# A row softmax bound by DMA: narrow loads of the first tile against a split load of the third

## The chip, the core and the metric

The kernel runs on one core of a Trainium2 chip. The metric is device time in microseconds of one execution. The core has a vector engine (DVE), a scalar engine (ACT), a sync engine (SP) that here issues every transfer, and sixteen DMA engines that all of SP's transfers share.

## The reference

A softmax with temperature over the last axis of a 16 x 256 x 32768 float32 array:

```python
def setup_inputs():
    batch, seq, vocab = 16, 256, 32768
    return {
        "logits": np.random.randn(batch, seq, vocab).astype(np.float32),
        "temperature": 1.0,
    }

def reference(logits: np.ndarray, temperature: float) -> np.ndarray:
    scaled = logits / temperature
    scaled = scaled - scaled.max(axis=-1, keepdims=True)
    exp_scaled = np.exp(scaled)
    return (exp_scaled / exp_scaled.sum(axis=-1, keepdims=True)).astype(np.float32)
```

512 MB are read and 512 MB are written.

## The kernel before

The 4096 rows of 32768 values are seen as 8192 half rows of 16384, so that a tile is 128 half rows, one to a partition, 64 KB each (8 MB in all), and two neighbouring partitions hold one row. There are 64 tiles and three buffers (`_BUFS`) for them in the on-chip memory `xs`; tile g uses buffer g mod 3, and it is loaded, worked on in place and stored from there.

**Work on a tile.** A tile is cut along its columns into three pieces of 6304, 5376 and 4704 columns (`_PLAIN`), the last two tiles into six (`_LATE`). `Work.vector` takes the negated maximum of each piece on DVE (L207). `Work.scalar` then does the exponential of each piece with that maximum as bias, and sums it (L267). A few small operations on DVE and ACT exchange maxima and sums between the two partitions of a row and make one factor per piece. The pieces are scaled with it, the first one on ACT (L286), the other two on DVE (L258).

**Order.** The program orders everything by hand with semaphores; no scheduler is involved. SP runs one list of loads and stores, written by `order`: load 0, 1, 2, store 0, load 3, store 1, store 2, then load i and store i-1 in turn, and at the end load 62, load 63, store 61, 62, 63. In front of a load into a buffer in use, SP waits until the store from that buffer has landed; in front of a store it waits for the scaling. SP issues in order, and what it issues goes through one queue to the sixteen DMA engines. Tiles 4 to 60 run on DVE and ACT in a loop over three buffers; the first four and the last three tiles are written out.

**Parts of transfers.** `load_parts` cuts the load of a tile by columns. Tile 0 is loaded in two parts: 15360 columns for all 128 partitions in one transfer (rows of 60 KB), and the last 1024 columns (`_NARROW`, 4 KB a row) in nineteen narrow transfers, given by `narrow_rows`: 18 transfers of seven partitions each (every 18th row) and one of the two rows left over. Tile 3 is loaded in two halves, since tile 0 is stored in two halves (`store_parts`); the last tile is stored in three parts. All other loads and stores are one transfer of 128 rows of 64 KB.

**Waits on loads.** Each transfer adds 16 to a semaphore of its part and buffer. `landed` waits on it before the first piece that touches a part: for part 1 of tile 0 the count of all nineteen narrow transfers. As the first and the fourth tile share the semaphore of part 1, the wait for tile 3 counts past those nineteen.

Of the kernel before, what the change touches and what calls it, by code (L numbers as in the profile page):

```python
# [8 lines left out]
_W = 16384  # L9
# [1 line left out]
_PLAIN = ((6304, 5376, 4704), (0,))  # L11
_LATE = ((4096, 3072, 3072, 2048, 2048, 2048), (3, 4, 5))
_LAST_STORES = ((0, 4096), (4096, 6144), (10240, 6144))
_NARROW = 1024
_FEW = 7
_HEAD = 4
_TAIL = 3

# [45 lines left out]


def load_parts(g):
    if g == 0:
        return [(0, _W - _NARROW), (_W - _NARROW, _NARROW)]
    if g == 3:
        return [(0, _W // 2), (_W // 2, _W // 2)]  # L70
    return [(0, _W)]


def store_parts(g, n):
    if g == 0:
        return [(0, _W // 2), (_W // 2, _W // 2)]
    return list(_LAST_STORES) if g == n - 1 else [(0, _W)]


def narrow_rows(p):  # L80
    step = p // _FEW
    return [slice(q, step * _FEW, step) for q in range(step)] + [slice(step * _FEW, p)]


def order(n):
# [7 lines left out]
def kernel(  # L93
# [6 lines left out]
    nc = tc.nc  # L100
    inv_t = 1.0 / float(temperature)
    P = nc.NUM_PARTITIONS
# [8 lines left out]
    x = xf.rearrange("n (h v) -> (n h) v", h=2)  # L111
# [8 lines left out]
    X = nc.alloc_sbuf_tensor("xs", [P, _BUFS * _W], fp32)  # L120
# [4 lines left out]
    sig = Signals(nc)  # L125
    stored = {}

    def load(g):
        p = Place(g, G)
        rows = slice(g * P, (g + 1) * P)  # L130
        for j, (s, n) in enumerate(load_parts(g)):
            if g >= _BUFS:
                parts = store_parts(g - _BUFS, G)
                for i, (a, m) in enumerate(parts):
                    if a < s + n and s < a + m:
                        nc.sync.wait_ge(*stored[g - _BUFS][i])
            where = slice(p.slot * _W + s, p.slot * _W + s + n)
            key = ("ld", j, *p.key)
            if g == 0 and j == 1:
                for some in narrow_rows(P):  # L140
                    sig.dma(key, nc.sync.dma_start(out=X[some, where], in_=x[some, s : s + n]))
            else:
                sig.dma(key, nc.sync.dma_start(out=X[:, where], in_=x[rows, s : s + n]))

# [19 lines left out]
    class Work:  # L164
# [25 lines left out]
        def landed(self, engine, k, seen):  # L190
            s, n = self.p.pieces[k]
            for j, (a, m) in enumerate(load_parts(self.p.g)):
                if a < s + n and s < a + m and j not in seen:
                    seen.add(j)
                    times = len(narrow_rows(P)) if self.p.g == 0 and j == 1 else 1
                    value = self.p.n16
                    if self.p.g == 3 and j == 1:
                        value, times = 16 * len(narrow_rows(P)) + 16, 1
                    engine.wait_ge(sig[("ld", j, *self.p.key)], value * times)

        def vector(self):
            t, e, r, tv, f, K = self.t, self.e, self.r, self.tv, self.j, self.K
# [85 lines left out]
    for what, g in order(G):  # L288
        if what == "L":
            load(g)  # L290
        else:
            store(g)
# [47 lines left out]
```

## Time and profile before

| | before |
|---|---|
| median of 3 runs | 2486.93 us (2486.84 to 2486.94) |
| profiled execution | 2486.8 us, its span 2485.0 us |
| DVE busy | 1526.2 us (61%) |
| ACT busy | 1325.7 us (53%) |
| DMA queue | 19264 packets, 1073.75 MB, 99.8% of sixteen engines |
| mean rate over the span | 432 GB/s |

The span is the time from the first to the last instruction that the profile shows; the execution's own time is some 2 us longer. The DMA share is the time that packets took, as a share of sixteen engines' time. In the rows of windows the columns are: the stretch and its length in us, the busy time of DVE, ACT and POOL with numbers of instructions, the TensorE clock (not used here), the DMA share and GB/s. A packet is one row's contiguous piece, carried by one DMA engine, and is counted in a window by its start, so that short windows scatter. In the rows of the timeline the columns are the start, the length, the engine, the line, the operation, and in brackets the idle time before it with what ended it.

### The profile page before, as it was taken

How to read it: one execution, taken by the hardware profiler on the slowest of the kernel's cores; microseconds unless marked ns; L12 is line 12 of the kernel's file. 1: busy time of each engine (PE TensorE's matmuls, PEld its weight loads, DVE VectorE, ACT ScalarE, POOL GpSimd, SP SyncE). 2: the span in 40 equal slices, each digit the busy share in tenths (PEclk: the TensorE clock that was granted, in tenths of full speed). 3: DMA queues.
4: the chain of work that ended last, by engine and by line, in shares of the span. 5: the costliest groups of instructions: out<-in, count | busy, mean ns of one | idle time of the engine just before them, and what ended most of it. 6: DMA issues, size and time to landing. Idle time of an engine off the chain costs nothing.

```text
span 2485.0 us, 1689 instructions
## 1 busy us (share of the span) xinstructions
DVE 1526.2 (61%) x776; ACT 1325.7 (53%) x529; POOL 0.2 (0%) x4
## 2 busy tenths in 40 slices
DVE  5845665666656656566565665656656566566665
ACT  4744645546546455464554645546455464554654
POOL 0000000000000000000000000000000000000000
DMA  9999999999999999999999999999999999999998
GB/s 399 438 439 432 429 438 437 430 434 437 437 427 437 437 434 429 438 438 429 434 437 436 428 437 438 433 430 438 437 428 436 437 435 428 438 437 434 430 438 381
DMA packets 19267, 1073.78 MB, mean 432 GB/s; under 512 B 2240, under 2 KB 2240, under 8 KB 2368
## 3 DMA queue, kind: packets, MB, share of 16 engines
q1 hardware_dynamic: 19264, 1073.75, 99.8%
q14 instruction: 3, 0.02, 0.0%
HBM read 536.87 MB, written 536.87 MB: 432 GB/s over the span
## 4 chain that ended last, share of the span: by engine, by line
DMA 61%; DVE 28%; ACT 7%; issue 2%; SPq 0%; DVEq 0%
DMA xs<-in_logits_dram 59%; DVE t L207 21%; ACT xs L267 6%; DVE xs L258 6%; DMA out_dram<-xs 3%; SPq L160 0%; ACT ee L278 0%; DVE junk L252 0%; DVE t L225 0%; DVE row L249 0%; ACT xs L286 0%; DVE row L229 0%; DVE junk L236 0%; DVEq L299 0%; DVEq L223 0%
## 5 line engine op out<-in xcount | busy, mean ns | idle before, releaser
L267 ACT ACTIVATE xs<-xs,t 128x6304 f32<-128x6304 f32 (+5 forms) x198 | 932.1, 4707 | 1053.6 <-DVE t L207 1046.8
L207 DVE TENSOR_REDUCE t<-xs 128x1 f32<-128x6304 f32 (+5 forms) x198 | 1110.0, 5663 | 618.5 <-DMA xs<-in_logits_dram 618.5
L286 ACT ACTIVATE xs<-xs,junk 128x6304 f32<-128x6304 f32 (+1 forms) x68 | 355.6, 5236 | 45.0 <-DVE junk L252 45.0
L258 DVE TENSOR_SCALAR xs<-xs,junk 128x5376 f32<-128x5376 f32 (+2 forms) x130 | 358.8, 2803 | 2.3
L225 DVE LOAD_MASK_SELECT t<-t x64 | 0.9, 14 | 282.9 <-ACT xs L267 282.9
L278 ACT ACTIVATE ee<-t,row 128x6 f32<-128x6 f32 (+1 forms) x64 | 19.2, 300 | 35.3 <-DVE row L229 35.3
L267 ACT ACTIVATION_READ_ACCUMULATOR xs<-xs,t 128x1 f32 x198 | 37.0, 187 | 0.0
L236 DVE CUSTOM_DVE_ANT_1 junk<-ee,t 128x6 f32<-128x6 f32 (+1 forms) x64 | 10.7, 167 | 23.5 <-ACT ee L278 23.5
L252 DVE TENSOR_SCALAR junk<-ee,row 128x3 f32<-128x3 f32 (+1 forms) x64 | 14.6, 229 | 2.2
L249 DVE RECIPROCAL row<-row 128x1 f32<-128x1 f32 x64 | 10.5, 164 | 2.2
L229 DVE TENSOR_REDUCE row<-t 128x1 f32<-128x6 f32 (+1 forms) x64 | 10.2, 159 | 2.2
L225 DVE STREAM_SHUFFLE t<-t 128x6 f32<-128x6 f32 (+1 forms) x64 | 10.4, 163 | 0.5
L236 DVE DVE_READ_ACCUMULATOR2_ANT row<- 128x1 f32 x64 | 5.3, 83 | 0.0
L267 ACT ACT_TABLE_LOAD x1 | 1.3, 1283 | 0.9 <-SPq L119 0.9
L321 POOL MEMSET const-bfloat16-1.0<- 128x1 bf16 x1 | 0.1, 102 | 0.0
L321 POOL MEMSET const-uint8-127<- 128x1 uint8 x1 | 0.1, 102 | 0.0
L321 POOL MEMSET const-float32-0.0<- 128x1 f32 x1 | 0.1, 99 | 0.2 <-issue 0.2
L321 POOL MEMSET const-float32-1.0<- 128x1 f32 x1 | 0.1, 99 | 0.0
## 6 DMA issues: line engine op xcount, KB each, us to landing
out_dram<-xs SPq DMA_DIRECT2D x2, 4096.0 KB, 29.2
xs<-in_logits_dram SPq DMA_DIRECT2D x2, 4096.0 KB, 19.3
xs<-in_logits_dram SPq DMA_DIRECT2D x1, 7680.0 KB, 21.1
out_dram<-xs SPq DMA_DIRECT2D x2, 3072.0 KB, 19.5
out_dram<-xs SPq DMA_DIRECT2D x1, 2048.0 KB, 12.2
xs<-in_logits_dram SPq DMA_DIRECT2D x62, 48.1
out_dram<-xs SPq DMA_DIRECT2D x62, 29.1
xs<-in_logits_dram SPq DMA_DIRECT2D x18, 28.0 KB
```

The source lines that it names most:

```text
L207: m = v.tensor_reduce(out=t[:, k : k + 1], in_=self.piece(k), axis=mybir.AxisListType.X, op=A.max, negate=True,)
L225: v.stream_shuffle(out=t[:, 2 * K : 4 * K], in_=t[:, 0 : 2 * K], mask=swap), "sh"
L229: v.tensor_reduce(out=r[:, 0:1], in_=tv[:, :, 0, :], axis=mybir.AxisListType.XY, op=A.min),
L236: v.tensor_tensor_reduce(out=f[:, 0 : 2 * K].rearrange("p (a k) -> p a k", a=2), in0=self.ev, in1=tv[:, :, 1, :], scale=1.0, scalar=0.0, o ...
L249: self.done(v.reciprocal(out=r[:, 2:3], in_=r[:, 1:2]), "rc")
L252: v.tensor_scalar_mul(out=f[:, 0:K], in0=e[:, 0:K], scalar1=r[:, 2:3]), "f"
L258: v.tensor_scalar_mul(out=xs, in0=xs, scalar1=f[:, k : k + 1]), k, self.p.own
L267: s = a.activation(out=xs, in_=xs, func=Exp, bias=t[:, k : k + 1], scale=inv_t, accum_out=t[:, K + k : K + k + 1],)
L278: a.activation(out=self.ev, in_=self.tv[:, :, 0, :], func=Exp, bias=r[:, 0:1], scale=-1.0),
L286: self.scaled(a.mul(out=xs, in_=xs, mul=f[:, k : k + 1]), k, self.p.on_act)
L321: nc = _bacc.Bacc("TRN2", target_bir_lowering=False, num_devices=1)
```

## The change

The whole of tile 0 is loaded in one transfer of 128 rows of 64 KB. Tile 2 is loaded in ten transfers in place of one: the left half of its columns for all 128 partitions in one transfer (rows of 32 KB); the right half in seven transfers of 16 partitions each (partitions r, r+8, r+16, ... for r from 0 to 6) and two of 8 partitions each (7, 15, ..., 63 and 71, 79, ..., 127). The first eight of them count as part 0, the last two as part 1, and each part has its semaphore. The maximum of tile 0 waits for the one transfer; the first piece of tile 2 waits for all ten. With the nineteen narrow transfers gone, the wait for part 1 of tile 3 is a plain 16.

```diff
-_NARROW = 1024
-_FEW = 7
+_SPLIT = 2
...
 def load_parts(g):
-    if g == 0:
-        return [(0, _W - _NARROW), (_W - _NARROW, _NARROW)]
+    if g == _SPLIT:
+        return [(0, _W), (0, _W)]
     if g == 3:
         return [(0, _W // 2), (_W // 2, _W // 2)]
     return [(0, _W)]
...
-def narrow_rows(p):
-    step = p // _FEW
-    return [slice(q, step * _FEW, step) for q in range(step)] + [slice(step * _FEW, p)]
...
             key = ("ld", j, *p.key)
-            if g == 0 and j == 1:
-                for some in narrow_rows(P):
-                    sig.dma(key, nc.sync.dma_start(out=X[some, where], in_=x[some, s : s + n]))
+            if g == _SPLIT:
+                half = _W // 2
+                b = p.slot * _W
+                parts = [(slice(0, P), 0)] + [(slice(r, P, 8), half) for r in range(7)]
+                if j == 1:
+                    parts = [(slice(7, P // 2, 8), half), (slice(P // 2 + 7, P, 8), half)]
+                for some, c in parts:
+                    sig.dma(
+                        key,
+                        nc.sync.dma_start(
+                            out=X[some, b + c : b + c + half], in_=x[rows, c : c + half][some]
+                        ),
+                    )
             else:
                 sig.dma(key, nc.sync.dma_start(out=X[:, where], in_=x[rows, s : s + n]))
...
                     seen.add(j)
-                    times = len(narrow_rows(P)) if self.p.g == 0 and j == 1 else 1
-                    value = self.p.n16
-                    if self.p.g == 3 and j == 1:
-                        value, times = 16 * len(narrow_rows(P)) + 16, 1
-                    engine.wait_ge(sig[("ld", j, *self.p.key)], value * times)
+                    value = 16 if j == 1 else self.p.n16
+                    value = [128, 32][j] if self.p.g == _SPLIT else value
+                    engine.wait_ge(sig[("ld", j, *self.p.key)], value)
```

## The prediction

> **What bounds the kernel now.** I read the page first: engine shares, DMA line, queue line.
>
> ```profile
> span 2485.0 us, 1689 instructions
> DVE 1526.2 (61%) x776; ACT 1325.7 (53%) x529; POOL 0.2 (0%) x4
> ...
> q1 hardware_dynamic: 19264, 1073.75, 99.8%
> ```
>
> No compute engine is near full; the one DMA queue fills 99.8% of sixteen engines' time. So the time is bytes through the DMA engines, plus what slows a packet, plus how unevenly the sixteen finish. The windows show where the first loss lies.
>
> ```profile
> 2.00:62.00 60.00, 35.02 (x14) 25.39 (x10) 0.00 (x0) 1.00 1.00 409
> 62.00:139.00 77.00, 59.99 (x35) 57.46 (x24) 0.00 (x0) 1.00 1.01 435
> ```
>
> The last column is GB/s. The first three loads run at 409, everything later at 435: 60 us x 26/435 = 3.6 us is lost before 62 us, and hardly anything after it. The windows of the end show the second loss.
>
> ```profile
> 2470.00:2477.00 7.00, 0.00 (x0) 0.00 (x0) 0.00 (x0) 1.00 1.04 446
> 2477.00:2478.00 1.00, 0.00 (x0) 0.00 (x0) 0.00 (x0) 1.00 0.40 172
> 2478.00:2480.00 2.00, 0.00 (x0) 0.00 (x0) 0.00 (x0) 1.00 0.40 172
> 2480.00:2482.00 2.00, 0.00 (x0) 0.00 (x0) 0.00 (x0) 1.00 0.12 49
> ```
>
> The column before GB/s is the DMA share. It falls to 0.40 and then 0.12 while the last bytes go out: nine engines are done near 2477.5, six between 2479.9 and 2481.3, one at 2483.3.
>
> For more I went to the trace's packet records (start, duration, size). They carry no engine number, but each packet starts 3 to 4 ns before another one ends, so they string into sixteen chains:
> - A 65536-byte packet takes 2418 ns, in nearly every case exactly; a 32768-byte one 1213 (512 of them, 1227 at most); a lone 4096-byte one 159; the 4-byte semaphore write behind each transfer 9. That fits 8 ns plus 36.8 ns per KB, and leaves 3.6 us per engine above the fit in all: 0.65 in the first packet of each engine, 2.45 between 21 and 34 us, 0.5 elsewhere.
> - The 2.45 us are the narrow stretch. The 128 packets of 4096 bytes lie on just seven chains, 18 or 19 on each. The first take 159 ns, then 250 to 340, and the nine other chains, which are already reading tile 1, need 3882 to 4279 ns for a 64 KB packet in that time. All returns to 2418 soon after the narrow ones end at 26 us.
> - The seven chains leave it some 2.9 us behind the nine, and this lag stays to the end, unchanged to some ns from tile to tile. One of the seven loses another 20 ns or so per transfer, 3.2 us up to the last ones, in steps of 3 to 11 ns a packet. This late engine is the one that ends at 2483.3 us, and 1.7 us later the span ends.
>
> So the kernel ends when the late engine has done its own packets; it is never idle between. The profiled execution took 2486.8 us for its span of 2485.0 (1.8 around it); the median of the runs is 2486.93, 0.1 more.
>
> **The change, part by part**, on the late engine's chain.
>
> *Bytes moved between engines.* Before, it carries 18 narrow packets and their semaphore writes, 18 x (159 + 5) = 2.95 us, less 8 x (2418 - 2267) = 1.21 us for tile 0's shorter main packets (61440 bytes): 1.74 us above a plain load. After, tile 2 gives every engine eight packets of 32 KB for the first half and one from each of the seven 16-row transfers; the two 8-row transfers have eight packets each. Few-row transfers of the trace all went to the same chains (the 18 of seven rows to the same seven, the one of two rows to two of them), so I put both on one group of eight that contains the seven. An engine of this group has 17 pieces: 9681 ns for the first eight with their semaphore write (the spacing of tile 3's halves) and 9 x 1214 = 10926, in all 20607 against 19317 for a plain load: 1.29 above. Difference: **-0.45 us**.
>
> [...]
>
> *The slow stretch.* On the seven chains it costs 18 x (265 - 159) = 1.9 us in the narrow packets and about 0.4 in the first packets of tile 1 behind them, 2.3 us. No 4096-byte piece is left. The new pieces are 32 KB; the nearest row is tile 3's half loads and tile 0's half stores at 1213 to 1227 ns, so I price their slowdown at nothing. The far bound is the worst factor of the stretch, 4200/2418 = 1.7 on all nine added pieces: 9 x 1213 x 0.7 = +7.6 us. Below nothing is excluded, 1213 being the lowest of 512. Tile 1 behind tile 0 may keep the 20 ns a packet that tile 0's later packets show above the fit: 0.15 us. So **-2.15 us**.
>
> *Issue on SP.* It goes from one DMA, nineteen narrow ones and two to two and ten.
>
> ```profile
> 0.96 0.38 SPq L143 DMA_DIRECT2D xs<-in_logits_dram  x1
> 1.41 13.83 SPq L141 DMA_DIRECT2D xs<-in_logits_dram  x19
> 15.28 0.82 SPq L143 DMA_DIRECT2D xs<-in_logits_dram  x2
> 50.84 0.82 SPq L160 DMA_DIRECT2D out_dram<-xs  x2
> ```
>
> Nineteen at 0.73 us become ten at no more than that: all is issued by 9 us, while tile 0's packets run to 22 us and tile 2's start near 41. Nothing waits for it, before or after: 0.
>
> *Tile 0 is waited for whole.* The first maximum on DVE now needs 64 KB a row in place of 60.
>
> ```profile
> 22.09 17.34 DVE L207 TENSOR_REDUCE t<-xs 128x1 f32<-128x6304 f32 x3 [22.09 <-DMA xs<-in_logits_dram]
> ```
>
> Eight packets of 2418 in place of 2267, less a little: DVE starts 0.9 us later, and as tiles 0 to 3 follow each other on DVE without a gap, the first stores come 0.9 us later: the pair at 50.84 becomes 51.8. The cover is the queue: the leading engines are busy with tile 2 until 62.0 us now and 59.8 then. That leaves 8 us; tile 2's store at 108 keeps 8 of about 11. With the cover gone the 0.9 us would be paid in full. Tile 2's own pieces are all waited for together, but DVE reaches that tile long after it has landed: 0.
>
> *The end.* The final stores are issued at 2457.04, a fixed chain of work after tile 62 has landed on the late engine. The leading nine stood idle for up to 0.39 us there; the late one had over 5 us of its own packets in hand. The chain moves with the late engine: 0.
>
> Sum: -0.45 - 2.15 = -2.6 us. Made on the profiled 2486.8, that gives 2484.2, with the 0.1 to the median **2484.3 us**, -0.10%. About 0.2% (5 us) is what a measurement of this kernel can tell from no change, so most of this forecast lies within "same".
>
> **The rivals.**
>
> *The slow stretch belongs to the step from tile 0 to tile 1, not to the small pieces.* For: the nine chains reading tile 1 slow down just as much. Against: it begins and ends with the narrow packets. Only the bytes are left, -0.45: 2486.5. Chance 0.13.
>
> *The slowdown is a price per transfer, whatever its size.* 2.3 us over 18 is 0.13 each; nine are added: +1.15, so 2485.5. For: each piece has a semaphore write behind it, and the gaps around these grew to some 10 to 30 ns in the stretch. Chance 0.11.
>
> *The two 8-row transfers fall elsewhere.* On different eights, each engine has 16 pieces and the late one ends 1.21 us sooner, 2483.1. If both miss the late engine, it gains 2.43 and the next one, 2.0 us ahead of it, sets the end: 2482.3, with the errors of the other terms perhaps beyond -0.2%. Against: the seven-row transfers never moved. Chance 0.08.
>
> *Slower: all sixteen engines in short pieces hinder each other.* In the stretch only seven alternated with semaphore writes and memory gave all of them 1.7 times the time; in tile 2 all sixteen do, in step, on rows 512 KB apart. At 1.24 times the added 32 KB packets (2.6/10.9) the gain is used up; at 1.7 it is +7.6 - 2.6 = +5.0, 2491.9. Against: 512 packets at 1213, in loads and stores with all engines active. Chance 0.06.
>
> *Slower: each transfer's fixed time is exposed.* From the last packet to the end of the span 1.7 us pass; were this paid nine times, 15.3 - 2.6 = +12.7: 2499.6. Against: nineteen narrow transfers passed in under 5 us, since transfers queue behind each other. Chance 0.02.
>
> [...]
>
> *The change does nothing it says:* excluded; the order of instructions on SP shows the ten transfers, and no other engine's order changes.
>
> **How the numbers follow.** The forecast has 0.60. The range from 2482.9 to 2486.8 holds it, both small-gain rivals and the better half of the uneven placement. Slower by over 0.2%: 0.06 + 0.02 = 0.08. Faster by over 0.2%: only the far end of the placement rival, 0.03; it takes a late engine that is free of both transfers. Same: 0.89.
>
> **What would show it.** Right: 4096-byte packets gone; tile 1's packets at 2418 from the first on; GB/s from 2 to 62 us near 425; eight chains behind the others by 2.4 us; first DVE work near 23.0; store issue near 51.8; late engine done near 2480.7. Wrong: 32 KB packets of tile 2 above 1250, slow packets at the start of tile 1, an idle gap on the late engine, or a steady packet other than 2418.

## The result and the profile after

The changed kernel takes 2494.8 us against 2486.65 of the kernel before in the same runs, 8.15 us more (medians of eight executions each); the ratio is 1.0037 (95% interval 1.0026 to 1.0048). The ratios in this text go nearer by the means, so single long executions raise them, as one of 2504.12 us does here beside seven from 2494.5 to 2495.0. The forecast was 2484.3, its range 2482.9 to 2486.8.

The page's head, then the windows of the first stretch, of the kernel after (columns as in the table of before; the last two are the DMA share and GB/s):

```profile
span 2493.0 us, 1680 instructions
DVE 1526.2 (61%) x776; ACT 1325.5 (53%) x529; POOL 0.2 (0%) x4
...
q1 hardware_dynamic: 19264, 1073.75, 99.9%
```

```profile
2.00:62.00 60.00, 34.28 (x14) 24.64 (x10) 0.00 (x0) 1.00 1.01 389
62.00:139.00 77.00, 60.73 (x35) 58.20 (x24) 0.00 (x0) 1.00 1.01 413
```

The same bytes, packets and compute, and again DMA engines that are never idle. What changed is the rate: 409 GB/s became 389 up to 62 us, where 425 was forecast, and the next window, full rate before, fell from 435 to 413. Cut finer, the place is plain:

```profile
2.00:21.00 19.00, 0.00 (x0) 0.18 (x1) 0.00 (x0) 1.00 1.01 428
21.00:31.00 10.00, 8.17 (x2) 1.42 (x1) 0.00 (x0) 1.00 0.97 419
31.00:50.00 19.00, 14.11 (x11) 17.76 (x8) 0.00 (x0) 1.00 0.98 426
50.00:70.00 20.00, 18.79 (x4) 13.17 (x6) 0.00 (x0) 1.00 1.01 231
```

The kernel before, in the second and the last of these windows:

```profile
21.00:31.00 10.00, 8.91 (x2) 2.15 (x1) 0.00 (x0) 1.00 1.08 366
50.00:70.00 20.00, 18.05 (x4) 13.18 (x6) 0.00 (x0) 1.00 1.00 434
```

Tiles 0 and 1 and the left half of tile 2 now run near full rate. From 50 to 70 us, where the transfers of 16 and 8 rows are, the rate is 231 GB/s with all engines busy: a packet takes twice its time. The packet records give the sizes. Most 32 KB pieces of the 16-row transfers take 2553 ns, not 1213. The two 8-row pieces of the eight lagging engines take about 2516 and 2248.

SP and DVE do what the forecast said, the first stores included:

```profile
0.94 0.86 SPq L147 DMA_DIRECT2D xs<-in_logits_dram  x2
1.84 6.22 SPq L142 DMA_DIRECT2D xs<-in_logits_dram  x10
51.58 0.83 SPq L164 DMA_DIRECT2D out_dram<-xs  x2
```

The windows of the end are those of before, 8 us later: two groups of engines, and one late engine.

```profile
2485.00:2486.00 1.00, 0.00 (x0) 0.00 (x0) 0.00 (x0) 1.00 0.52 221
2486.00:2488.00 2.00, 0.00 (x0) 0.00 (x0) 0.00 (x0) 1.00 0.46 197
2488.00:2490.00 2.00, 0.00 (x0) 0.00 (x0) 0.00 (x0) 1.00 0.17 74
2490.00:2493.00 3.00, 0.00 (x0) 0.00 (x0) 0.00 (x0) 1.00 0.02 8
```

Below, **excess** is packet time above the fit of the prediction (8 ns plus some 36.8 ns per KB, a KB being 1000 bytes there and 1024 elsewhere in this text, so that 65536 bytes take 2418 ns), summed and divided by sixteen engines, of the one profiled execution of each kernel; **later excess** is that from 85 to 2450 us. Before: 3.6 us in all, 2.46 of it between 20 and 41 us, 0.04 from 41 to 85, 0.27 later. After: 11.9 in all, 0.01, 10.14 and 0.97 there. The first stretch was indeed cleared, and four times as much was put in.

### The profile page after: what moved, and what is told of

Its sections match the earlier page's. It is cut to its first block, busy times and chain, and to the rows that moved or that the text cites. A ratio compares the mean times of both kernels' runs of the same rounds, so it can differ in the third digit from the quotient of the medians.

```text
span 2493.0 us, 1680 instructions
## 1 busy us (share of the span) xinstructions
DVE 1526.2 (61%) x776; ACT 1325.5 (53%) x529; POOL 0.2 (0%) x4
## 2 busy tenths in 40 slices
DMA packets 19267, 1073.78 MB, mean 431 GB/s; under 512 B 2240, under 2 KB 2240, under 8 KB 2240
## 4 chain that ended last, share of the span: by engine, by line
DMA 62%; DVE 28%; ACT 7%; issue 2%; SPq 0%; DVEq 0%
DMA xs<-in_logits_dram 58%; DVE t L209 21%; ACT xs L269 6%; DVE xs L260 6%; DMA out_dram<-xs 3%; SPq L164 0%; ACT ee L280 0%; DVE junk L254 0%; DVE t L227 0%; DVE row L251 0%; ACT xs L288 0%; DVE row L231 0%; DVE junk L238 0%; DVEq L301 0%; DVEq L225 0%
```

## The experiments

The edits are shown shortened. Those of e5 and e12 are made to the kernel before, all others to the changed kernel. Three theories stood at the start. P: the partitions decide, that is, which of them the engines write at the same time. S: short pieces with a semaphore write behind each are slow by themselves. H: rows 512 KB apart in memory are slow.

### e1_plain: neither narrow loads nor split load

```diff
-        return [(0, _W), (0, _W)]            # tile 2: ten transfers
+        return [(0, _W)]                     # tile 2: one transfer of 128 rows
```

> Tile 0 and tile 2 are both loaded in one transfer of 128 rows: neither the narrow loads nor the split load. All theories that blame the pieces agree: tile 1's packets and tile 2's take 2418 ns from the first on, all sixteen engines stay within some 0.8 us of each other but for the late one, and by the prediction's own terms (1.74 us of unevenness and 2.15 us of slow packets gone) the time is 2486.65 - 3.9 = 2482.8 us. If the slow stretch of before belonged to the step from tile 0 to tile 1, it is still there and the time is near 2484.9.

Measured: 2487.06 us, ratio to before 1.0007 (0.9997 to 1.0017). The stretch behind tile 0 is gone (excess 0.01 from 20 to 41 us), so it belongs to the narrow pieces and not to the step from tile 0 to tile 1. But 2482.8 did not come. The excess moved: 1.25 us at the end of tile 2's load, and 4.44 us later. Its windows, against those of before:

```profile
50.00:70.00 20.00, 18.84 (x4) 13.18 (x6) 0.00 (x0) 1.00 0.97 393
```

```profile
139.00:500.00 361.00, 212.48 (x108) 183.95 (x72) 0.00 (x0) 1.00 1.00 432
```

The kernel before in that second window:

```profile
139.00:500.00 361.00, 213.28 (x108) 184.77 (x72) 0.00 (x0) 1.00 1.00 435
```

3 of 435 GB/s over 361 us is 2.5 us, in a stretch with no odd transfer at all. The packet records show where: at 58.4 us all sixteen engines start their last packet of tile 2, with a store behind it, and all of them take 0.8 to 1.3 us too long; near 195 us, at the end of a store, each takes another 0.2 to 0.8 us. Each such loss pushes the engines apart: within 0.6 us of each other at 62 us, they stand in bands at 0, 2.4 and 4.2 us behind by 2 ms, and the loss fades. This gave theory T: sixteen engines that switch between load and store together lose time, and a lag between groups (the time by which one group of engines trails the other) avoids that. By T the narrow loads of before bought something with their 2.3 us.

### e2_short_rows, e3_blocks, e4_near_rows: what makes a piece slow

```diff
 # tile 2's right half, [(partitions, rows of memory, first column, columns)]
+e2: [(all, all, H + 1024 * i, 1024) for i in range(8)]
+e3: [(16r .. 16r+15, the same rows, H, H) for r in range(8)]
+e4: [(r, r+8, r+16 .., rows 16r .. 16r+15, H, H) for r in range(8)]
```

> [...] Theory S (short pieces with a semaphore write behind them hinder each other): 250 to 340 ns for each of 64 packets, +6 to +11 us: 2489 to 2494. [...]

> Tile 2's right half comes in eight transfers of 16 neighbouring partitions and rows, 32 KB each, one piece for each engine as in the changed kernel. [...] Theory S: the pieces are as short as in the changed kernel, 2553 ns each: 8 x 1.34 = +10.7, 2493.5. Theory H: the sixteen rows are now 64 KB apart in memory in place of 512 KB, so the pieces come down towards 1213: 2483.

> As the changed kernel's 16-row transfers (eight of them, partitions r, r+8, r+16, ...), but read from 16 neighbouring rows of memory, so that the rows of tile 2's right half lie in other partitions than they belong to and this half of the tile is not the reference's. [...] Theory H: the rows are 64 KB apart, 1213 ns, 2483. Theory S: 2553 ns, 2493.5.

Measured, one run each: e2 2487.0, e3 2509.45, e4 2495.87 us. The piece times, more than these single totals, carry the reading. The windows of 50 to 70 us, e2 first:

```profile
50.00:70.00 20.00, 18.92 (x4) 13.18 (x6) 0.00 (x0) 1.00 1.01 410
```

then e3, which needs the next window too:

```profile
50.00:70.00 20.00, 19.03 (x4) 13.18 (x6) 0.00 (x0) 1.00 1.07 147
70.00:100.00 30.00, 20.15 (x12) 16.11 (x7) 0.00 (x0) 1.00 0.97 283
```

and e4:

```profile
50.00:70.00 20.00, 18.92 (x4) 13.18 (x6) 0.00 (x0) 1.00 1.03 224
```

e2's 1024 packets of 4 KB (eight transfers of 128 rows) have a median of 159 ns, its rate is no lower than the plain kernel's (393), and its time is the plain kernel's, 3.6 us above an estimated 2483.4 (e1's forecast of 2482.8, with 56 further packets an engine at the 8 ns of the fit or a little more): shortness is nothing. (A 128-row transfer has sixteen semaphore writes for its 128 packets: the 2240 of the changed kernel's trace are sixteen for each of 139 transfers and eight for each of the two of 8 rows. The other half of S is tested by e5 and e8.) e4 reads neighbouring rows into the partitions of the changed kernel, and its pieces take 2548 ns: the distance of the rows in memory (64 KB in place of 512) is nothing, and H falls. e3 has neighbouring rows in neighbouring partitions, pieces as short and as many as e4, and takes 4169 ns a piece. Only the partitions differ in a way that orders the three, as P has it. P gives no size, though, and why a block of sixteen takes 1.6 times as long as steps of 8 (4169 against 2548 ns) is not shown.

### e7_strides: steps of 4 and of 2

```diff
+    [every fourth of partitions 0 to 63] * 4, [every second of a block of 32 in 64 to 127] * 4
```

> Tile 2's right half in eight transfers of 16 rows: the first four take every fourth partition of 0 to 63, the last four every second of a block of 32 in 64 to 127. [...] Rival D (the nearer the partitions, the slower; 2553 at step 8, 4171 at step 1): some 3000 ns at step 4 and 3500 at step 2, 2502. Rival F (each side of 64 partitions has a rate of its own): twice 2553 on one side, 2516.

Measured: 2496.24 us (one run). Its window is that of steps of 8:

```profile
50.00:70.00 20.00, 18.82 (x4) 13.18 (x6) 0.00 (x0) 1.00 1.02 221
```

The slow pieces have a median of 2547 ns at steps 4 and 2, against 2553 at step 8. D had asked for 3000 and 3500 ns, F for twice 2553 on one side of 64: between steps of 2 and 8 neither distance nor side matters. The block of sixteen neighbours (e3, 4169 ns) stands apart, and no run shows what sets it apart. In e3 the engines start a piece at times up to 2.6 us apart; what a piece takes when they start together was not tested.

### e5_own_port: the narrow loads of tile 0 in sixteen transfers of eight rows

```diff
-    step = p // _FEW
-    return [slice(q, step * _FEW, step) for q in range(step)] + [slice(step * _FEW, p)]
+    return [slice(c + q, c + 32, 4) for c in (64, 96, 0, 32) for q in range(4)]
```

> The kernel before, but with its narrow loads of tile 0 (4 KB a row) in sixteen transfers of eight rows in place of nineteen: partitions 64 to 127 first, then 0 to 63, each transfer taking every fourth of 32 partitions. Eight rows go to eight engines. [...] Theory S or a price of each transfer: all sixteen pieces at 250 to 340 ns, about 2486.3. Theory T (sixteen engines that switch from loads to stores together lose up to 1.2 us at a switch, and a lag between two groups avoids it): the lag is 2.6 us, so no slow packets later, under 0.5 us from 150 us on.

Measured: 2486.53 us, ratio 1.0007 (0.9993 to 1.0021). The pieces differ within one run: once the other engines are at tile 1, those of the first eight transfers (partitions 64 to 127) take 298 to 338 ns; those of the last eight (0 to 63) come down through 200 to 159 while the others are still loading tile 1. Each of these pieces has its own semaphore write behind it, so the rest of S falls, too. The first tile 1 packet of the other eight takes 3611 to 3687 ns in place of 3882 to 4279, the next one 2418 to 2427. So what was slow in the narrow stretch of before was not the 4 KB. By P it was the partitions; as they went in this order, the run does not separate them from the place in the list. The excess there fell from 2.46 to 1.28 us. The time did not follow, as 2.67 us of later excess came with it, against 0.27, although there was a lag of 2.4 us between groups of eight and eight (before: 2.8 us, nine and seven). Which of the two makes the difference was not tested. Theory T's "under 0.5" is wrong here.

### e6_even: the change without its lag

```diff
-                if j == 1:
-                    parts = [(slice(7, P // 2, 8), half), (slice(P // 2 + 7, P, 8), half)]
+                # r runs to 7: an eighth transfer of 16 rows in place of two of 8
```

> The changed kernel with tile 2's right half in eight transfers of 16 rows, the last two of 8 rows joined to one, so that no group of engines lags. Theory P: all eight pieces take 2553 ns, +10.7 us above a slow-free plain load. Theory T: without the lag the engines lose 3 to 4 us more at later switches, as in the plain kernel, so 2495.9, as with the rows from near memory. Rival (the later loss of the plain kernel has nothing to do with the lag): no loss later, 2492.5.

Measured: 2495.6 us, ratio 1.0038 (1.0023 to 1.0052). Excess 9.91 from 41 to 85 us and 3.15 later, against 10.14 and 0.97 in the changed kernel: the same slow pieces, and without the lag 2.2 us more later, as T has it.

### e8_after_t2, e9_half, e10_more_lag: the lag without the stretch

```diff
+    some = [slice(c + q, c + 32, 4) for c in (64, 96, 0, 32) for q in range(4)]
+    return [(every, every, 0, _W - w)] + [(q, q, _W - w, w) for q in some]   # tile 2; w = 1024, 512, 1536
```

> No narrow loads at tile 0; at the end of tile 2's load sixteen narrow transfers of eight rows of 4 KB, every fourth of 32 partitions as in the run before. Behind tile 2 the other eight engines go on to a store, which reads these partitions. [...] If the lag is no help (rival to T): some 4 us of later loss, 2487 to 2488.

> As the run before with rows of 2 KB: half the lag, 1.3 us. Theory T with a lag that need only exceed the time of one switch (1.2 us): no later loss, and 0.7 us less on the late engine: 2483.5. If the lag is too small: part of the plain kernel's loss returns, 1 to 4 us, 2484.5 to 2487. Rival (the lag is no help): as the run before, 0.7 us less, 2486 to 2487.

> The narrow transfers of eight rows behind tile 2 with rows of 6 KB in place of 4: the lag of the eight engines is 3.9 us in place of 2.6, near the 4.5 us of the changed kernel. Theory T (a wider lag keeps the groups apart): the 0.94 us that the 4 KB kernel still lost between 200 and 300 us is gone, for 0.65 us more on the late engine: 2485.9 against 2486.1. If the lag beyond some 3 us is no help, 2486.8. The loss of 0.94 us at the first step from loads to stores stays in both, since the lag begins only there.

Measured: e8 2486.11 us, ratio 1.0014 (0.9993 to 1.0034); e9 2486.53, ratio 1.0004 (0.9994 to 1.0015); e10 2497.7, ratio 1.0046 (1.0018 to 1.0074), with single runs from 2486.15 to 2516.57. In e8 the pieces behind tile 2 take 159 ns after the first three or four, with the other engines at a store at that time; the first eight of e5, in the same order beside a load, took 298 to 338. So a store beside them did not slow these pieces as a load did in e5, and P holds, if at all, for writes alone. e8's time lies between an estimated 2484.1 for no later loss (by the packet times of before the late engine carries 1.41 us above a plain load in place of 4.04) and the 2487 to 2488 for no help from the lag. Its excess is 0.94 at the first step from load to store and 1.22 later; e9, with rows half as long, has 1.45 and 1.99. e10 contradicts the simple form of T. In its profiled execution the lag of 3.4 us grew to over 8 and the rate stayed low to the end:

```profile
139.00:1000.00 861.00, 517.98 (x255) 447.04 (x173) 0.00 (x0) 1.00 1.00 432
1000.00:2000.00 1000.00, 605.30 (x310) 524.20 (x204) 0.00 (x0) 1.00 1.00 429
```

against 435 and 434 in the kernel before. Why it does so in some executions and stays near 2486.5 in others is open. The width of the lag is not enough to explain it: the changed kernel's is 4.5 us and more with a later excess of 0.97, and e1, which has no such groups, has one execution of 2502.73 us among its twelve. Six of e10's twelve are above 2500 us; of the kernel before, none of 86 is above 2487.89.

### e11_seven_t2: the narrow loads of before, behind tile 2

```diff
+    some = [slice(q, 126, 18) for q in range(18)] + [slice(126, P)]
+    return [(every, every, 0, _W - 1024)] + [(q, q, _W - 1024, 1024) for q in some]   # tile 2
```

> The narrow transfers of the kernel before, 18 of seven rows and one of two, as they were (4 KB a row, every 18th partition), but behind tile 2's load in place of tile 0's; tile 0 is loaded whole. [...] Theory P with reads apart from writes: pieces at 159 ns but for the first few, no slow stretch of 2.3 us; the first step from loads to stores without a lag costs some 0.9 us on all engines; the lag of 2.9 us keeps the later loss under 0.3 us as before: 2486.75 - 2.3 + 0.9 = 2485.4. If short pieces are slow by themselves: 280 ns each, 2487.5. If the lag must be there from tile 0 on: 1 to 4 us of later loss, 2486.5 to 2489.

Measured: 2485.28 us against 2486.83, ratio 0.9995 (0.9986 to 1.0004). The same nineteen transfers that cost 2.46 us of excess behind tile 0 cost next to nothing beside a store: the excess is 0.00 from 20 to 41 us, 0.82 from 41 to 85, 0.72 later (under 0.3 had been expected). This is the lowest median of all, 1.55 us or 0.06% below the kernel before; the interval includes no change.

### e12_both: the added part alone

```diff
 # the kernel before, and
+            if g == 2:   # the changed kernel's ten transfers
```

> The added part of the change alone: the kernel before with its narrow loads of tile 0, and tile 2 loaded in the changed kernel's ten transfers as well. Theory P: the pieces cost what they cost in the changed kernel, 7 x 1.34 + some 1.6 for the two 8-row ones, on top of everything that before has: 2486.75 + 11 = 2497.7, or some us less where the two groups, 2.9 us apart by then, do not write at the same time. The lag adds up to some 7 us; if a lag as wide as that loses by itself, as the kernel with 6 KB rows did in part of its runs, 2504 to 2517.

Measured: 2513.94 us, ratio 1.0125 (1.0092 to 1.0159), single runs from 2502.59 to 2525.93. In the profiled one (2502.6) the excess from 41 to 85 us is 11.42 in place of 0.04: the split of tile 2 alone costs 11 us there, on top of the narrow stretch (2.28). Its window, against 434 GB/s in the kernel before:

```profile
50.00:70.00 20.00, 17.90 (x4) 13.18 (x6) 0.00 (x0) 1.00 1.02 241
```

Another 3.73 came later, with a lag of some 5 us; that this is the loss of e10 is not shown.

## Why the prediction was wrong

- **The slow stretch of before: right in size and place, not in cause.** All of its 2.3 us went when the 4 KB pieces left tile 0: 2.46 us of excess became 0.01, and tile 1's packets take 2418 ns from the start. Its rivals fell: without pieces there is no slow step to tile 1 (e1), and more transfers alone cost nothing (e2). But the prediction counted it as gone because no 4096-byte piece was left; by e5 it was not their length that made it (298 to 338 ns in the first eight transfers, down to 159 in the last eight), and the new pieces, at eight times the length, were slow again (2553 ns in place of 1213).
- **Bytes, issue and start: right.** Eight chains lag, with two pieces more than the others, though by 4.5 us (2.4 forecast), as these pieces are slow too; all is issued at 8.1 us (9 forecast); DVE starts at 22.83 (23.0); the first stores are issued at 51.58 (51.8).
- **The step that failed: "I price their slowdown at nothing."** On one of the eight lagging engines the nine added pieces, with the packets at either end, took about 11.0 us more than 1213 ns a piece, by e2, e3 and e4 because of the partitions that they went to. With the other terms, -0.45 - 2.15 + 11.0 = +8.4; the late engine ended at 2491.3 in place of 2483.3, +8.0. The remaining 0.4 was not traced.
- **Why it was priced so.** The row was chosen by length: 32 KB pieces of 128-row transfers. What decided was which partitions were written at the same time. The 128-row transfers of before run at full rate (2418 ns for 64 KB, 1213 for 32 KB), and no row of before shows anything else but the narrow stretch. That stretch was the nearest row; I used it as the far bound only. Even so the bound was low, 7.6 us against 11.0: it took the 1.7 times of the 64 KB packets for the worst factor, while the 4 KB pieces in the same list went from 159 to 340 ns, 2.1 times, and 9 x 1213 x 1.1 is 12.0 us.
- **The rival that came true.** "All sixteen engines in short pieces hinder each other" had the place, the sign and the point from which it decides (1.24 times; 2.1 came). Its reason is refuted: shortness by e2, semaphore writes by the 159 ns pieces of e5 and e8, the distance of the rows by e4. It had 0.06.
- **A second error, hidden by the first.** The sum took the lag as a pure cost. Without it, e1 lost 4.44 us later, and the plain kernel came out level with before, 4.3 us above the 2482.8 worked out from the same terms. The changed kernel keeps a lag, so this does not show in its time; the gain of taking the narrow loads away would not have come by that alone.

## What to carry to other kernels

Before a load is cut by partitions, write down which partitions are written at the same time, and measure a piece: here sixteen rows of 32 KB at steps of 2, 4 or 8 ran at half rate (2547 to 2553 ns in place of 1213) and a block of sixteen at under a third (4169), while a cut by columns over all 128 partitions cost nothing that showed (e2, 2487.0 us against 2487.06). A few short transfers on some engines only cost least where the other engines were at a store (e11: 0.82 us of excess there, against 2.46 behind tile 0). And when a kernel is bound by DMA with every engine busy, read the packet times by stage: an odd-looking load may be what spares a later loss (0.27 us of later excess in the kernel before, 4.44 in e1).

## What was not expected of the hardware

- Sixteen engines that wrote 32 KB each into partitions at steps of 8 took 2553 ns, a little worse than half the rate of 1213; into a block of sixteen neighbours 4169 ns, with the engines up to 2.6 us out of step.
- With the other engines at a store, 4 KB pieces took 159 ns after the first three or four (e8); with them at a load, the first eight of the same list took 298 to 338 (e5).
- Sixteen engines that went from a load to a store within a microsecond lost about 1.2 us, each in one packet. The two groups of the kernel before, 2.8 us apart, did not (0.04 us there); e5's and e8's, 2.4 to 3 us apart, lost 1.2 to 2.7 us later. In e10's profiled execution the lag grew past 5 us and the rate stayed low to the end; single executions were up to 30 us longer. What costs the time at such a switch is open, and T with it.
